# Accumulating DMAs in the FFN of a two-layer hybrid block: y's middle sums and the low part of w_down

## The chip, the cores and the metric

The kernel runs on one core of a Trainium2 chip. The metric is the device time of one execution in microseconds (us). Before the change the median of three runs is 1789.37 us (1785.97 to 1790.05). One core has five engines with queues of their own: TensorE (PE, with its weight loads as PEld), VectorE (DVE), ScalarE (ACT), GpSimd (POOL) and SyncE (SP). DMAs are issued from a queue, in this kernel from SP's and POOL's, and are carried out by 16 DMA engines that all queues share.

## The reference

Two layers work on a main stream x (512 tokens of width 1024) and, in layer 0, on a context stream (256 tokens). Each layer has a mixing part (attention, a Fourier mix and a long convolution) and then the feed-forward part that the change touches:

```python
def conv_ffn(h, w_up, w_c, b_c, w_down):
    u = dwconv3(h @ w_up, w_c, b_c)
    gate, val = jnp.split(u, 2, axis=-1)
    return (jax.nn.silu(gate) * val) @ w_down

fx = rmsnorm(x, g_pre_ffn[i]) * (1.0 + sc2) + sh2
yx = conv_ffn(fx, w_up[i], w_ffn_conv[i], b_ffn_conv[i], w_down[i])
x = x + ga2 * rmsnorm(yx, g_post_ffn[i])
```

`w_up` is 1024 x 5632, `w_down` 2816 x 1024, all in float32. The context stream has the same FFN in layer 0 alone.

## The kernel before

**High and low parts.** A float32 operand of a matmul is split into two tiles of a rounded type (F32R): the high part is the rounded value, the low part the remainder. `split` (lines 179 to 183) does this with a cast on ACT (L181) and a subtraction on DVE or POOL (L182). `mm3` (L196, L197, L198) adds three products into PSUM: high by high, high by low, low by high. `load_w` (L189) loads 512 KB of weights from DRAM to a tile `Wr` on SP's queue and splits it into `Wh` and `Wl`.

**The FFN's loops.** The hidden width is 22 chunks of 128. Per chunk m, the up-projection makes the gate and the value, a convolution over neighbouring tokens follows (`conv3`, L636 to L638), then SiLU on ACT, the product `ft` on POOL (L1229, L1335), and a split into `gc` or `gT`. In the main stream (`ffn_x`) the up-projection is a Strassen-like scheme of seven products. `prep` loads two `w_up` tiles `r` and makes four sums on POOL (`tt`, L1276 to L1279), which are then split into `Wh`, `Wl` and an M tile. In the context stream (`ffn_c`) the `w_up` tiles are split directly (`L`).

**The down-projection.** `ffn_down` takes the chunks in groups of two (the last group of the main stream has four). It loads a group's `w_down` chunks with `load_w`, and for each tile t of 128 tokens it multiplies the group into a PSUM pair `pw` (128 x 1024). The sum over all groups stands in the SBUF tile y[t]: the first group is copied there by ACT (L1200), each middle group is added by DVE (L1202), and the last one is added by halves (L1196), followed by the squares for the norm and the tail (residual, store). A group's down-projection is emitted after the first chunk of the next group. For the context stream the low parts of `w_down` are made on POOL (`CE = True`), for the main stream on DVE: 22 chunks for the context stream and 22 for each layer of the main stream, 66 in all. There are 82 middle sums.

**What sets the order.** In Python, generators yield estimated costs, and a planner (`go`, `pump`, `need`) mixes filler work, such as the modulation matmuls with `w_mod`, into the main work. A scheduler then fixes each engine's own order when the program is built, with a model of time (`schedule_with_timeline_sim=True`, L1698). On the chip each queue runs in that order, and an instruction that waits holds up all behind it on its engine.

**Buffers.** Tiles of one tag share a fixed count of buffers, and a new tile waits until an old one has been read for the last time:

```python
BUFS = {"M": 27, "T": 5, "Q": 3, "L": 3, "Wr": 2, "Wh": 4, "Wl": 4, "Wm": 3}
```

`M` holds y, gT, the Strassen sums and other tiles of 128 x 1024. PSUM has two pairs `pw` and four banks `pn`.

Of the kernel before, what the change touches and what calls it, by code (L numbers as in the profile page):

```python
# [8 lines left out]
F32 = mybir.dt.float32  # L9
F32R = mybir.dt.float32r  # L10
I32 = mybir.dt.int32
AF = mybir.ActivationFunctionType
ALU = mybir.AluOpType
# [4 lines left out]
P = 128  # L18
# [50 lines left out]
class Net:  # L69
# [115 lines left out]
    def load_w(self, src, shape=None, el=None, tag=None, raw=None):  # L185
        shape = shape or [P, 1024]
        r = self.tl(shape, F32, raw or tag or "Wr")
        for i, a in enumerate(src if isinstance(src, list) else [src]):
            self.nc.sync.dma_start(r[:, 2 * i : 2 * i + 2] if isinstance(src, list) else r, a)  # L189
        h, lo = self.tl(shape, F32R, tag or "Wh"), self.tl(shape, F32R, tag or "Wl")  # L190
        self.split(h, lo, r, el)
        return h, lo

    def mm3(self, ps, l, r, first, last, **kw):
# [970 lines left out]
    def ffn_down(self, l, st, g, ms, begin, el=None, early=0, mid=None):  # L1165

        nc = self.nc
        end = ms[-1] == MF - 1
        if begin and st is self.X:
            st.y = [self.M("y", F32) for _ in range(st.NT)]  # L1170
        wd = {k: self.load_w(self.I["w_down"][l, k], el=nc.gpsimd if el else None) for k in ms}
        if end:
            ss = [self.small("ss", 2, 6) for _ in range(st.NT)]
            xr = [self.load_r(self.src[st.name][t]) for t in range(st.NT)]
        acc = {}

        def add(t, h, ks):
            hs, ts = slice(h * 512, (h + 1) * 512), slice(t * P, (t + 1) * P)
            if (t, h) not in acc:
                if h == 0:  # L1180
                    acc[t] = self.pw()
                acc[t, h] = acc[t][:, hs]
            for k in ks:
                self.mm3(acc[t, h], (g[k][:, 0, ts], g[k][:, 1, ts]), (wd[k][0][:, hs], wd[k][1][:, hs]), k == ms[0], k == ms[-1])
            yield 3 * len(ks) * C512, 0.0

        for t in range(early):
            for h in range(2):
                yield from add(t, h, ms[:-1])
        for t in range(st.NT):  # L1190
            y = st.y[t]
            for h in range(2):
                hs = slice(h * 512, (h + 1) * 512)
                yield from add(t, h, ms[-1:] if t < early else ms)
                if end:
                    nc.vector.tensor_tensor(y[:, hs], y[:, hs], acc[t, h], op=ALU.add)  # L1196
                    self.sumsq_half(ss[t], y[:, hs], h)
                    nc.gpsimd.tensor_tensor(y[:, hs], y[:, hs], st.G[1][:, hs], op=ALU.mult)
            if begin:
                nc.scalar.copy(y, acc[t])  # L1200
            elif not end:
                nc.vector.tensor_tensor(y, y, acc[t], op=ALU.add)  # L1202
            else:
                self.tail(st, t, xr[t], ss[t])
                if t == Z["MT"] and mid:
                    yield from mid
# [495 lines left out]
```

## Time and profile before

| | before |
|---|---|
| median of three runs | 1789.37 us |
| profiled execution | 1784.91 us |
| its span (first to last instruction) | 1783.1 us |
| PE busy | 1639.1 us (92%) |
| DVE busy | 1440.1 us (81%) |
| ACT busy | 934.9 us (52%) |
| POOL busy | 692.3 us (39%) |
| DMA queues, share of 16 engines | SP and others 35.6%, POOL 5.5% |

A group row of the profile names the line, engine, operation and tiles (written <- read), the shapes and the count; then busy us and mean ns of one; then the idle time of the engine just before, with what ended it. A wait row names who waited, for whom, total us, times and the longest. A row of a table by stretches has for each engine busy us and count, then TensorE's granted clock, the share of the DMA engines and GB/s. DMA issue rows end with the median us from issue to landing. Rows of the table of DMA queues give packets, MB and the time of the packets as a share of 16 engines' span.

### The profile page before, as it was taken

The page shows a single profiled execution, that of the slowest core. Times are in us where ns is not written, and L with a number is a line of the kernel's source. Part 1 is how long each engine was busy: PE and PEld are TensorE (multiplying, and loading weights), DVE is VectorE, ACT ScalarE, POOL GpSimd, SP SyncE. Part 2 cuts the span into 40 slices and gives each one's busy share as a digit, 9 for nine tenths or more (in the row PEclk, how much of TensorE's full clock was granted, in tenths as well). Part 3 has the DMA queues.
Part 4 walks back from the last instruction along what each step waited for, and adds up shares of the span by engine and source line. Part 5 has one row for each costly group of instructions (what it writes and reads, how often), then busy time and mean ns, then how long its engine had stood idle before and what let it go on. Part 6 is the DMA issues. An engine that isn't in the chain of part 4 may idle for free. (4 is left out here: it accounts for less than half of the span.)

```text
span 1783.1 us, 27842 instructions
## 1 busy us (share of the span) xinstructions
PE 1639.1 (92%) x10502; PEld 1397.4 (78%) x10502; DVE 1440.1 (81%) x2324; ACT 934.9 (52%) x1737; POOL 692.3 (39%) x515
## 2 busy tenths in 40 slices
PE   5799987899999997989999998998898799999997
PEld 2677775687788897878989885787787678889996
DVE  5888777697665688889988987668895878999997
ACT  2642344487565454556554556434773465555454
POOL 3343332000134337665554645212002455655543
PEclk9899999999999998999999999999999899999999
DMA  9214277603477642332342258653012343332323
GB/s 366 101 61 146 86 243 263 232 13 130 162 253 232 228 155 71 96 118 84 101 148 84 89 185 305 213 175 118 1 48 83 130 146 103 95 107 86 127 62 119
DMA packets 70003, 248.01 MB, mean 139 GB/s; under 512 B 8111, under 2 KB 9647, under 8 KB 69868
## 3 DMA queue, kind: packets, MB, share of 16 engines
q1 hardware_dynamic: 60716, 215.54, 35.6%
q0 software_dynamic: 9152, 30.68, 5.5%
q8 instruction: 83, 1.36, 0.3%
q14 instruction: 52, 0.43, 0.1%
HBM read 232.03 MB, written 14.16 MB: 138 GB/s over the span
## 5 line engine op out<-in xcount | busy, mean ns | idle before, releaser
L196 PE MATMUL pn<-h,Wh 128*128 128x256 f32 x1328 | 376.6, 286 | 11.7 <-DVE ft L638 4.3
L198 PE MATMUL pn<-h,Wl 128*128 128x256 f32 x1328 | 372.8, 284 | 10.2 <-DVE Wl L182 10.2
L197 PE MATMUL pn<-h,Wh 128*128 128x256 f32 x1328 | 374.2, 283 | 1.7 <-POOL h L182 1.7
L196 PEld LDWEIGHTS pn<-h,Wh 128*128 128x128 f32 x1328 | 253.2, 191 | 24.5 <-issue 7.8
L198 PEld LDWEIGHTS pn<-h,Wl 128*128 128x128 f32 x1328 | 252.1, 191 | 15.3 <-DVE Wl L182 12.7
L197 PEld LDWEIGHTS pn<-h,Wh 128*128 128x128 f32 x1328 | 253.8, 191 | 6.2 <-POOL h L182 2.4
L181 ACT CAST Wh<-Wr 128x1024 fp32r<-128x1024 f32 x118 | 122.7, 1049 | 138.9 <-PE pw L198 46.4
L182 DVE TENSOR_TENSOR Wl<-Wr,Wh 128x1024 fp32r<-128x1024 f32 x89 | 129.7, 1465 | 53.7 <-ACT Wh L181 53.2
L1276 POOL TENSOR_TENSOR tt<-r,r 128x512 f32<-128x512 f32 x44 | 75.0, 1705 | 233.9 <-DMA r<-w_up 211.0
L196 PE MATMUL pw<-Wh,gT 128*128 128x512 f32 x352 | 137.5, 404 | 9.0 <-ACT gT L181 3.9
L197 PE MATMUL pw<-Wl,gT 128*128 128x512 f32 x352 | 138.5, 396 | 3.1 <-DVE Wl L182 3.1
L198 PE MATMUL pw<-Wh,gT 128*128 128x512 f32 x352 | 137.8, 396 | 1.8 <-DVE gT L182 1.8
L181 ACT CAST Wh<-tt 128x1024 fp32r<-128x1024 f32 x88 | 90.8, 1048 | 84.9 <-PE pn L197 42.4
L182 DVE TENSOR_TENSOR Wl<-tt,Wh 128x1024 fp32r<-128x1024 f32 x88 | 122.5, 1411 | 11.0 <-ACT Wh L181 8.0
L1335 POOL TENSOR_TENSOR ft<-ft,ft 128x512 f32<-128x512 f32 x44 | 70.8, 1609 | 132.4 <-DVE ft L638 94.2
L1202 DVE TENSOR_TENSOR y<-y,pw 128x1024 f32<-128x1024 f32 x82 | 99.2, 1213 | 20.1 <-PE pw L198 20.0
L182 POOL TENSOR_TENSOR h<-tf,h 128x256 fp32r<-128x256 f32 (+1 forms) x40 | 36.0, 921 | 187.8 <-ACT h L181 186.5
L182 POOL TENSOR_TENSOR Wl<-Wr,Wh 128x1024 fp32r<-128x1024 f32 x29 | 74.6, 2578 | 57.7 <-ACT Wh L181 56.5
L1278 POOL TENSOR_TENSOR tt<-r,tt 128x512 f32<-128x512 f32 x44 | 75.8, 1722 | 51.9 <-DVE Wl L182 51.9
L196 PE MATMUL pw<-h,Wh 128*128 128x256 f32 (+1 forms) x224 | 76.9, 343 | 13.9 <-DVE v L638 2.6
L283 PE MATMUL pn<-wm,cpad 128*32 128x256 f32 x768 | 67.6, 411 | 19.7 <-DMA wm<-w_mod 19.3
L636 ACT ACTIVATE ft<-C,vec 128x512 f32<-128x512 f32 x88 | 68.7, 811 | 32.1 <-DVE C L1325 25.7
(361 smaller groups left out, 4706.1 us busy)
## 6 DMA issues: line engine op xcount, KB each, us to landing
wm<-w_mod SPq DMA_DIRECT2D x96, 512.0 KB, 5.4
r<-w_up SPq DMA_DIRECT2D x90, 512.0 KB, 3.6
Wr<-w_down SPq DMA_DIRECT2D x66, 512.0 KB, 3.8
L<-w_up SPq DMA_DIRECT2D x44, 512.0 KB, 4.4
Wr<-w_out SPq DMA_DIRECT2D x24, 512.0 KB, 3.6
Wr<-w_in_t SPq DMA_DIRECT2D x16, 512.0 KB, 3.9
dft<-hdft_x POOLq DMA_DIRECT2D x16, 512.0 KB, 4.1
Wr<-w_in_c SPq DMA_DIRECT2D x12, 512.0 KB, 3.6
```

The costliest lines, as they stand in the source:

```text
L181: r = nc.scalar.copy(hi, src)
L182: (el or nc.vector).tensor_tensor(lo, src, f32(hi), op=ALU.subtract)
L196: nc.tensor.matmul(ps, l[0], r[0], start=first, stop=False, **kw)
L197: nc.tensor.matmul(ps, l[0], r[1], start=False, stop=False, **kw)
L198: nc.tensor.matmul(ps, l[1], r[0], start=False, stop=last, **kw)
L283: nc.tensor.matmul(ps[32 * g : 32 * g + 32, cs], self.cpad[:, q % 2 * 4 + g, :], w[:, g, :], start=q % 2 == 0, stop=q % 2 == 1, skip_group ...
L636: nc.scalar.activation(dst, ps, AF.Identity, scale=w1, bias=b)
L1202: nc.vector.tensor_tensor(y, y, acc[t], op=ALU.add)
L1276: te.tensor_tensor(half(t13, 0), half(r[1], 0), half(r[0], 0), op=ALU.subtract)
L1278: te.tensor_tensor(half(t24, 0), half(r[1], 1), half(t13, 0), op=ALU.subtract)
L1335: nc.gpsimd.tensor_tensor(o[0], o[0], o[1], op=ALU.mult)
```

## The change

Two things are changed in `ffn_down`, for both streams and both layers.

The weights `w_down` are loaded by a new helper, `load_w_acc`. It loads `Wr` as before on SP's queue. ACT then writes the negated, rounded weights to the low tile, and casts the weights to the high tile. A DMA issued on POOL's queue reads the same weights from DRAM a second time and adds them to the low tile, which then holds the weights less the high part. The subtraction on DVE or POOL is gone, so the argument that chose its engine is gone too.

The middle groups' sums are no longer added to y by DVE. ACT copies the PSUM pair to a new M tile `ya`, and a DMA on POOL's queue adds that tile to y, from SBUF to SBUF. The first and last groups stay as they were.

```diff
+    def load_w_acc(self, src):
+
+        nc = self.nc
+        r = self.tl([P, 1024], F32, "Wr")
+        nc.sync.dma_start(r, src)
+        h, lo = self.tl([P, 1024], F32R, "Wh"), self.tl([P, 1024], F32R, "Wl")
+        nc.scalar.activation(lo, r, AF.Copy, scale=-1.0)
+        nc.scalar.copy(h, r)
+        nc.gpsimd.dma_start(lo, src, accum_op=ALU.add)
+        return h, lo
...
-        wd = {k: self.load_w(self.I["w_down"][l, k], el=nc.gpsimd if el else None) for k in ms}
+        wd = {k: self.load_w_acc(self.I["w_down"][l, k]) for k in ms}
...
             if begin:
                 nc.scalar.copy(y, acc[t])
             elif not end:
-                nc.vector.tensor_tensor(y, y, acc[t], op=ALU.add)
+
+                part = self.M("ya", F32)
+                nc.scalar.copy(part, acc[t])
+                nc.gpsimd.dma_start(y, part, accum_op=ALU.add)
             else:
                 self.tail(st, t, xr[t], ss[t])
```

## The prediction

> **What bounds the kernel now.** I began with the stages, because the change touches only the two feed-forward parts. The view of busy time by stretch has, after the stretch and its length, busy us with instruction counts of PE, PEld, DVE, ACT and POOL, then granted clock, DMA share and GB/s. The context stream's FFN lies in 460 to 700 us, the main stream's in 740 to 1090 (layer 0) and 1405 to 1783 (layer 1).
>
> ```profile
> 490.00:624.00 134.00, 134.00 (x970) 116.06 (x969) 85.02 (x127) 73.44 (x113) 52.19 (x35) 1.00 0.71 238
> 740.00:1090.00 350.00, 334.40 (x2214) 298.29 (x2214) 304.92 (x391) 192.15 (x312) 190.12 (x124) 0.99 0.40 133
> 1450.00:1750.00 300.00, 292.38 (x2012) 267.97 (x2012) 270.68 (x297) 160.74 (x250) 155.02 (x93) 0.99 0.33 106
> ```
>
> PE is busy 100%, 96% and 97% of these stretches at a granted clock of 0.99 or 1.00. The timeline says that this is real issue and not only modelled ends: consecutive 256-column matmuls start every 0.12 us.
>
> ```profile
> 1519.74 0.28 PE L197 MATMUL pn<-h,Wh 128*128 128x256 f32 x1
> 1519.86 0.28 PE L198 MATMUL pn<-h,Wl 128*128 128x256 f32 x1
> 1519.98 0.28 PE L196 MATMUL pn<-h,Wh 128*128 128x256 f32 x1
> ```
>
> DVE is the second load (85 of 134, 305 of 350, 271 of 300), ACT and POOL are near half. So relief of DVE is worth only what PE waits for DVE. The waits of PE in the three stages (total us, times, longest), one block of rows a stage in the order 460 to 700, 740 to 1090, 1405 to 1783:
>
> ```profile
> PE pn L196 <- DVE ft L638: 4.3, 1, 4.3
> PE pn L198 <- DVE Wl L182: 2.9, 2, 1.6
> ...
> PE pw L196 <- ACT gT L181: 3.1, 3, 2.0
> PE pw L197 <- DVE Wl L182: 3.1, 2, 2.0
> PE pn L198 <- DVE Wl L182: 2.4, 4, 1.0
> PE pw L198 <- DVE gT L182: 0.9, 1, 0.9
> ...
> PE pn L198 <- DVE Wl L182: 4.1, 3, 2.5
> PE pw L196 <- DVE y L1196: 1.7, 2, 1.2
> PE pn L196 <- DVE C L1323: 1.1, 3, 0.7
> ```
>
> Waits of PE that end with DVE in these rows sum to 4.3 + 2.9 + 3.1 + 2.4 + 0.9 + 4.1 + 1.7 + 1.1 = 20.5 us. That is the largest direct gain that I can point to.
>
> **The change, part by part.** What it takes away and what it adds is priced from these groups (busy us, mean ns of one; two windows for the subtraction of the main stream, one for the context stream):
>
> ```profile
> L182 DVE TENSOR_TENSOR Wl<-Wr,Wh 128x1024 fp32r<-128x1024 f32 x22 | 36.7, 1677 | 2.9 <-ACT Wh L181 2.9
> L182 DVE TENSOR_TENSOR Wl<-Wr,Wh 128x1024 fp32r<-128x1024 f32 x22 | 36.9, 1697 | 0.5 <-ACT Wh L181 0.4
> L182 POOL TENSOR_TENSOR Wl<-Wr,Wh 128x1024 fp32r<-128x1024 f32 x20 | 51.3, 2573 | 46.7 <-ACT Wh L181 46.5
> L1202 DVE TENSOR_TENSOR y<-y,pw 128x1024 f32<-128x1024 f32 x82 | 99.2, 1213 | 20.1 <-PE pw L198 20.0
> L181 ACT CAST Wh<-Wr 128x1024 fp32r<-128x1024 f32 x118 | 122.7, 1049 | 138.9 <-PE pw L198 46.4
> L1200 ACT COPY y<-pw x10: 1002/1008/1017, 508.7 to 1470.7; 128x1024 f32<-128x1024 f32 x10
> L716 POOL DMA_DIRECT2D dft<-hdft_x x16 | 9.5, 597 | 50.1 <-PE pn L198 43.6 <-DVE dec L750 3.6 <-PE pn L791 0.8
> Wr<-w_down SPq DMA_DIRECT2D x66, 512.0 KB, 3.8
> dft<-hdft_x POOLq DMA_DIRECT2D x16, 512.0 KB, 4.1
> ```
>
> - DVE loses 44 subtractions and 82 additions, 73.6 + 99.2 = 173 us of its 1440. POOL loses 22 subtractions of 2.57 us (57 us) and gains 66 + 82 = 148 DMA issues of 0.60 us (88 us). ACT gains 66 negated copies of 1.05 us and 82 copies out of PSUM of 1.01 us, 152 us, which puts it near 70% in the FFN.
> - **DVE's relief.** At most the 20.5 us above; those waits also have other causes in the same chains (the cast ahead of Wl, the POOL product ahead of gT), so I take half: −10 us (bounds −21 and 0).
> - **y's middle sums.** The PSUM pair was freed after an addition of 1.21 us and is now freed after a copy of 1.01 us: nothing lost there. The DMA behind it has a whole group (some 30 us) until y is touched again, so its landing costs 0. It waits on POOL for ACT's copy. Queued behind it are the four `tt` operations of the next weights and the product `ft`, for which ACT's cast of gT waits and then PE. POOL has idle time there before the first of these, so I take 0; without that cover it is at most 82 waits of one copy, 82 x 1.01 = 83 us:
>
> ```profile
> L1276 POOL TENSOR_TENSOR tt<-r,r 128x512 f32<-128x512 f32 x44 | 75.0, 1705 | 233.9 <-DMA r<-w_up 211.0
> L1335 POOL TENSOR_TENSOR ft<-ft,ft 128x512 f32<-128x512 f32 x44 | 70.8, 1609 | 132.4 <-DVE ft L638 94.2
> ```
>
> (`part` holds one of the 27 M buffers for a copy and a landing, some 5 us; whether one is free is not shown, I take 0 inside the same bound.)
>
> - **w_down's low part** is the term that decides. Before it was made by a subtraction behind the cast; now it is a negated copy, an issue in POOL's queue, and a landing. One group in layer 1, main stream:
>
> ```profile
> 1547.62 1.06 ACT L181 CAST Wh<-Wr 128x1024 fp32r<-128x1024 f32 x1
> ...
> 1548.36 2.24 POOL L1276 TENSOR_TENSOR tt<-r,r 128x512 f32<-128x512 f32 x1 [3.72 <-DVE Wl L182]
> ...
> 1550.04 1.65 DVE L182 TENSOR_TENSOR Wl<-Wr,Wh 128x1024 fp32r<-128x1024 f32 x1
> ...
> 1552.89 0.40 PE L197 MATMUL pw<-Wl,gT 128*128 128x512 f32 x1
> ```
>
> Before, Wl is ready at 1551.69 and PE reads it at 1552.89, 1.2 us later. After, the negated copy ends at 1548.68, POOL is in a `tt` until 1550.60, and a plain 512 KB load issued by POOL lands 4.1 us after its issue starts: 1554.7, or 1.8 us after PE used it. An accumulating DMA has to read the destination too. No row shows one. Its lower bound is the plain load; its upper bound is two plain passes. The size of a pass follows from the DMA table:
>
> ```profile
> q1 hardware_dynamic: 60716, 215.54, 35.6%
> q0 software_dynamic: 9152, 30.68, 5.5%
> ```
>
> POOL's queue took 5.5% of 1783 us, 98 us of all 16 engines, for 30.68 MB, so 0.524 MB take 1.7 us. With a second pass Wl is late by 1.8 + 1.7 = 3.5 us. I take the middle, 2.65 us. PE does other matmuls meanwhile: in the group shown it ran products of the next weights between its first matmul on the new Wh and that on Wl. But those products need buffers too: Wh and Wl have four each, a down group keeps two of them some 20 us, and ACT already waits for them (138.9 us before the casts in the group above). So a longer stay is partly paid later, by casts that start late. I take half of 2.65 us for each of 20 down groups of the main stream (ten a layer): +27 us (bounds 0 and 20 x 3.5 = 70). In the context stream PE never idled between 490 and 624 us, and the subtraction that falls away there cost 2.57 us itself; I take 0 for its latency, and the same 11 x 3.5 = 39 us as upper bound.
>
> - **DMA load in the context stream.** 20 chunks of w_down and 16 middle sums fall into 460 to 700 us:
>
> ```profile
> L181 ACT CAST Wh<-Wr x20: 1046/1048/1057, 494.1 to 672.1; 128x1024 fp32r<-128x1024 f32 x20
> L1202 DVE TENSOR_TENSOR y<-y,pw 128x1024 f32<-128x1024 f32 x16 | 19.5, 1219 | 6.9 <-PE pw L198 6.8
> ```
>
> That is 36 DMAs more, 60 us of all engines by one pass, spread over 240 us: +0.25 of the share, +0.50 by two passes. In 490 to 624 us the share is 0.71 already, so it becomes 0.96 to 1.21, 1.085 in the middle. What is over 1.00 lengthens the 134 us: 0.085 x 134 = +11 us (bounds 0 and 28). What is late next there is `L`, the w_up loads. In the main stream 0.40 and 0.33 leave room: 0.
>
> By the Trainium skill, "Collectives: The Full Stack", section "The bandwidth ceiling: the fold count and why AG ≠ RS ≠ AR", an adding transfer runs at half the rate of a copy, since each chunk needs two reads on one ring and the addition itself is free. By that rule the delay would be 3.5 us and the terms +35 and +28 in place of +27 and +11, an estimate 25 us higher; no trace here shows it.
>
> **The sum.** −10 + 27 + 11 = +28 us. The profiled execution took 1784.9 us (its span is 1783.1, 1.8 us lie around it), so 1813 us. The median of the runs shown is 4.5 us above that execution; the sum put on the median would be 1817, and I name 1815.
>
> **The rivals.**
>
> *Faster: the latency is covered and DVE's relief is left.* The scheduler that writes the order knows a DMA takes time and can put the loads ahead. Place: the pair Wl of w_down. It decides if PE has at least 3 us of `pn` products at hand for each group, which the timeline of the group above supports; the buffers' waits speak against. Price: all of DVE's 20.5 us with nothing paid, and 5 to 10 us more from DVE operations that no longer run beside each other: 1789 − 21 = 1768 to 1789 − 10 = 1779; I name 1774.
>
> *No difference: PE bound.* PE issues at its rate in 96% and more of these stretches. Then neither the 173 us that DVE loses nor a delay of 2 to 3 us reaches the end. 1789 us.
>
> *Much slower: an accumulating DMA lands as late as the slow loads in POOL's queue.* The four reloads of `h` landed after 8.3 to 14.1 us:
>
> ```profile
> h<-spill_h POOLq DMA_DIRECT2D x4, 512.0 KB, 11.1
> ```
>
> With 11.1 in place of 4.1 us, Wl is late by 8.8 us in each group. Half of it over 20 groups is 88 us, half over the 11 groups of the context stream 48 us, and the DMA load adds its upper 28 us: 1789 + 164 − 10 = 1943 at worst, and 1789 + 88 + 11 − 10 = 1878 if PE, always at work in the context stream, hides that stream's part. Those four loads came in one burst, which speaks against it.
>
> *The change does not do what it says*, if the addition were carried out by several small transfers or on POOL itself. Then POOL's issue would be longer than 0.6 us; at 1.7 us (a `tt`) 148 issues are 163 us more on an engine that is idle nearly half of the FFN: it ends within the much slower case.
>
> **How the numbers follow.** A measurement of this kernel tells apart about 0.2%, 3.6 us. Chances: forecast 0.45 (own range 1797 to 1843: between a third of the delay paid with no DMA overload, 1789 − 10 + 18, and all of it, 1789 − 10 + 53 + 11), much slower with its variants 0.18, faster 0.26, no difference 0.11. Slower by over 0.2% is 0.45 + 0.18 = 0.63, same 0.11, faster 0.26. Against the sum speaks that only PE decides, for it that every added step stands in a chain whose slack is 1.2 us. The range takes in the faster case's 1768 and the milder half of the much slower one, 1880: about 0.1 is left out on either side.
>
> **What would show it.** In the changed profile: waits of PE on a DMA into Wl (right if 10 us or more in all, wrong if none); the landing of the accumulating DMA from DRAM between 4.1 and 5.8 us, and POOL's issue near 0.6 us; the DMA share of the context stream at 0.95 or more, and waits for `L` there; DVE's busy time near 1440 − 173 = 1267 us or somewhat lower, ACT's near 1087; the stretch of the main stream's FFN longer in both layers. The forecast is wrong if PE's busy share in those stretches stays at 96% or more and their length does not grow, or if most of a loss sits in POOL's `ft`, behind y's DMAs, which I priced at 0.

## The result and the profile after

| | before | after |
|---|---|---|
| median | 1788.56 us | 1938.85 us (1931.65 to 1943.01) |
| ratio to before, 95% interval | | 1.0838 [1.0801, 1.0875] |
| span of the profiled execution | 1783.1 us | 1929.9 us |

The kernel is 8.4% slower. Forecast were 1815 us in a range of 1768 to 1880: the direction came out, the size did not. In the changed kernel the lines stand some ten further down: the matmuls L196, L197, L198 are now L207, L208, L209, the negated copy is L200, the cast of `w_down` L201, its accumulating DMA L202, y's copy L1215 and y's DMA L1216. The split stays at L181 and L182.

The page of after, its engines and its DMA queues:

```profile
PE 1685.2 (87%) x10502; PEld 1429.8 (74%) x10502; DVE 1302.5 (67%) x2198; ACT 1069.5 (55%) x1885; POOL 715.7 (37%) x641
...
q1 hardware_dynamic: 60716, 215.54, 31.6%
q0 software_dynamic: 30464, 108.29, 27.0%
```

PE was busy 92% of the span and is now busy 87%. DVE lost 138 us (1440 to 1302), less than the 173 forecast, and POOL's queue moves 108 MB in place of 31.

Where the time went is seen from marks that both kernels have (the first store of x, the last `w_up` split of the context stream, the stores of layer 0, the last store). The context stream's FFN grew from 223.0 to 255.1 us, the main stream's from 392.7 to 458.1 (layer 0) and 411.9 to 462.2 (layer 1). The mixing part between the two stayed (285.2 and 283.9). So the three FFN stages hold the whole difference: 32 + 65 + 50 = 147 us. The waits of PE in after (us in total, times, longest):

```profile
PE pw L208 <- DMA Wl<-w_down: 101.7, 34, 7.0
PE pn L294 <- DMA wm<-w_mod: 22.1, 16, 5.4
PE pn L207 <- ACT Wh L181: 10.6, 10, 2.1
...
PE pn L209 <- DVE Wl L182: 7.7, 8, 4.2
```

The first row answers the row `PE pw L197 <- DVE Wl L182` of before, 3.1 us in the three stages. 34 times PE stood for 3 us on average before the low part of `w_down`. The stretches (after the length: busy us of PE, PEld, DVE, ACT, POOL, then granted clock, DMA share, GB/s), which answer the three at the head of the prediction:

```profile
490.00:635.00 145.00, 129.27 (x896) 110.04 (x895) 65.55 (x107) 84.45 (x124) 33.93 (x40) 0.95 0.93 275
740.00:1180.00 440.00, 375.94 (x2433) 335.47 (x2432) 268.51 (x349) 256.09 (x381) 227.53 (x187) 0.93 0.69 177
1500.00:1900.00 400.00, 348.45 (x2286) 312.46 (x2286) 261.60 (x296) 234.43 (x341) 209.97 (x166) 0.94 0.67 168
```

PE's share is 89%, 85% and 87% where it was 100%, 96% and 97%; the granted clock went from 0.99 or 1.00 to 0.93 to 0.95; and the DMA share of the main stream rose from 0.40 and 0.33 to 0.69 and 0.67. The landings in after, median us in the last column:

```profile
r<-w_up SPq DMA_DIRECT2D x90, 512.0 KB, 5.9
y<-ya POOLq DMA_DIRECT2D x82, 512.0 KB, 6.0
Wr<-w_down SPq DMA_DIRECT2D x66, 512.0 KB, 6.6
Wl<-w_down POOLq DMA_DIRECT2D x66, 512.0 KB, 7.9
L<-w_up SPq DMA_DIRECT2D x44, 512.0 KB, 7.4
```

### The profile page after: what moved, and what is told of

It reads as the page before. It is cut to its first block, busy times and chain, and to the rows that moved or that the text cites. A ratio compares the mean times of both kernels' runs of the same rounds, so it can differ in the third digit from the quotient of the medians.

```text
span 1929.9 us, 28251 instructions
## 1 busy us (share of the span) xinstructions
PE 1685.2 (87%) x10502; PEld 1429.8 (74%) x10502; DVE 1302.5 (67%) x2198; ACT 1069.5 (55%) x1885; POOL 715.7 (37%) x641
## 5 line engine op out<-in xcount | busy, mean ns | idle before, releaser
L207 PE MATMUL pn<-h,Wh 128*128 128x256 f32 x1328 | 382.9, 290 | 17.4 <-ACT Wh L181 10.6
L209 PE MATMUL pn<-h,Wl 128*128 128x256 f32 x1328 | 376.0, 289 | 7.8 <-DVE Wl L182 7.7
L208 PE MATMUL pn<-h,Wh 128*128 128x256 f32 x1328 | 378.7, 287 | 1.7 <-POOL h L182 1.7
L207 PEld LDWEIGHTS pn<-h,Wh 128*128 128x128 f32 x1328 | 260.0, 196 | 29.7 <-ACT Wh L181 13.8
L209 PEld LDWEIGHTS pn<-h,Wl 128*128 128x128 f32 x1328 | 257.7, 197 | 15.0 <-DVE Wl L182 10.0
L208 PEld LDWEIGHTS pn<-h,Wh 128*128 128x128 f32 x1328 | 259.4, 195 | 6.4 <-POOL h L182 2.0
L208 PE MATMUL pw<-Wl,gT 128*128 128x512 f32 x352 | 150.0, 426 | 78.7 <-DMA Wl<-w_down 78.7
L182 DVE TENSOR_TENSOR Wl<-tt,Wh 128x1024 fp32r<-128x1024 f32 x88 | 126.2, 1440 | 41.1 <-ACT Wh L181 41.1
L207 PE MATMUL pw<-Wh,gT 128*128 128x512 f32 x352 | 144.4, 419 | 3.9 <-DVE y L1207 1.9
L209 PE MATMUL pw<-Wh,gT 128*128 128x512 f32 x352 | 146.3, 417 | 0.0
L208 PEld LDWEIGHTS pw<-Wl,gT 128*128 128x128 f32 x352 | 69.8, 198 | 98.6 <-DMA Wl<-w_down 84.1
L1215 ACT COPY ya<-pw 128x1024 f32<-128x1024 f32 x82 | 82.7, 1012 | 81.2 <-PE pw L209 81.0
L181 ACT CAST Wh<-tt 128x1024 fp32r<-128x1024 f32 x88 | 91.8, 1050 | 54.3 <-POOL tt L1293 37.7
L182 DVE TENSOR_TENSOR Wl<-r,Wh 128x1024 fp32r<-128x1024 f32 x40 | 70.2, 1754 | 68.6 <-ACT Wh L181 68.5
L648 DVE SCALAR_TENSOR_TENSOR ft<-C,vec,ft 128x511 f32<-128x511 f32 x88 | 84.8, 992 | 37.7 <-ACT ft L647 37.7
L649 DVE SCALAR_TENSOR_TENSOR ft<-C,vec,ft 128x511 f32<-128x511 f32 x88 | 107.0, 1251 | 0.2
L182 POOL TENSOR_TENSOR h<-tf,h 128x256 fp32r<-128x256 f32 (+1 forms) x40 | 37.5, 958 | 187.0 <-ACT h L181 183.1
L1216 POOL DMA_DIRECT2D y<-ya x82 | 74.3, 933 | 84.9 <-ACT ya L1215 71.5
L182 DVE TENSOR_TENSOR Wl<-L,Wh 128x1024 fp32r<-128x1024 f32 x44 | 58.3, 1326 | 68.3 <-ACT Wh L181 68.2
L181 ACT CAST Wh<-Wr 128x1024 fp32r<-128x1024 f32 x52 | 54.3, 1050 | 85.8 <-PE pw L209 45.6
L182 DVE TENSOR_TENSOR Wl<-Wr,Wh 128x1024 fp32r<-128x1024 f32 x45 | 56.1, 1249 | 50.4 <-ACT Wh L181 50.1
```

The costliest lines, as they stand in the source:

```text
L181: r = nc.scalar.copy(hi, src)
L182: (el or nc.vector).tensor_tensor(lo, src, f32(hi), op=ALU.subtract)
L207: nc.tensor.matmul(ps, l[0], r[0], start=first, stop=False, **kw)
L208: nc.tensor.matmul(ps, l[0], r[1], start=False, stop=False, **kw)
L209: nc.tensor.matmul(ps, l[1], r[0], start=False, stop=last, **kw)
L648: nc.vector.scalar_tensor_tensor(dst[:, 1:T], ps[:, 0 : T - 1], w0, dst[:, 1:T], op0=ALU.mult, op1=ALU.add)
```

## Experiments

Four explanations were set against each other: the low part lands late and nothing covers it; the added transfers and issues load the DMA engines and POOL; ACT's added copies cost; the four `Wh` and four `Wl` buffers turn round more slowly.

### Which part of the change

y's sums alone (`w_down` as before):

```diff
-        wd = {k: self.load_w_acc(...) for k in ms}
+        wd = {k: self.load_w(..., el=nc.gpsimd if el else None) for k in ms}
```

> Only y's middle sums go through ACT's copy and the accumulating DMA; w_down's low part is made by the subtraction as before. Theory A (PE waits for w_down's late low part, and little else costs): between -10 and +20 us against the kernel before, no wait of PE on a DMA into Wl. Theory B (the load of the 148 accumulating DMAs and of the copies on DMA engines, ACT and POOL): 82 of 148 DMAs, so some +80 us of the +146.

Measured 1813.58 us, 1.0128 [1.0098, 1.0157]. And `w_down`'s low part alone (y's sums by DVE as before):

```diff
-                part = self.M("ya", F32)
-                nc.scalar.copy(part, acc[t])
-                nc.gpsimd.dma_start(y, part, accum_op=ALU.add)
+                nc.vector.tensor_tensor(y, y, acc[t], op=ALU.add)
```

> Only w_down's low part is made by the negated copy and the accumulating DMA; y is summed by DVE as before. Theory A: +120 to +150 us, with PE's waits on the DMA into Wl near the 102 us of the changed kernel. Theory B: 66 of 148 DMAs, some +65 us.

Measured 1940.15 us, 1.0839 [1.0795, 1.0884]: as much as the whole change. So `w_down`'s part alone is enough for a loss of this size, and y's part, which costs 25 us alone, adds nothing to the total. By the marks the two runs are not the same, though: `w_down` alone has 237.4 us in the context stage and 464.8 and 475.6 in the main ones, where the whole change has 255.1, 458.1 and 462.2. y's sums on top cost 18 us in the context stage and give 20 back in the main ones; that these cancel is luck. Waits of PE in the run with y's sums alone:

```profile
PE pn L209 <- DVE Wl L182: 19.8, 18, 5.7
...
PE pw L207 <- ACT ya L1215: 9.7, 13, 2.0
```

No wait of PE on y's DMA is among them. The PSUM pair is now freed by ACT's copy, and PE waits for that 13 times; the waits of this kind for DVE's `Wl` have doubled (10.2 us, 10 times, in the whole run of before). y's copy without its DMA (the middle sums are then missing in y):

```diff
                 nc.scalar.copy(part, acc[t])
-                nc.gpsimd.dma_start(y, part, accum_op=ALU.add)
```

> The kernel with y's sums alone changed, without the accumulating DMA: ACT copies the middle groups' sums to the M tile and they are dropped (the middle sums are left out of y). If the +25 us of y's change come from the DMAs (issue, waits in POOL's queue, DMA engines): 0 to -15 us against the kernel before, since DVE's 99 us are gone. If they come from ACT's copy in the path that frees the PSUM pair: +15 to +30 us.

Measured 1803.65 us, 1.0076 [1.0053, 1.0098]. About 13 us of the 25 are there with the copy alone, although DVE has lost its 82 additions and has nothing in their place.

### Accumulating or plain

The same kernel with a plain DMA into the low tile, so that the high part is not subtracted:

```diff
-        nc.gpsimd.dma_start(lo, src, accum_op=ALU.add)
+        nc.gpsimd.dma_start(lo, src)
```

> As the kernel with w_down's low part alone changed, but the DMA of POOL's queue writes the weights over the low tile in place of adding them (the low tile then holds the whole weights, so the subtraction of the high part is left out). Same places in every queue, no second read. Theory A: the landing falls from 5.3 us at best to about 4 us, PE's waits on Wl fall by that much in each of some 34 waits, so 40 to 60 us less than with the addition, but still slower than before. Theory B: the share of the DMA engines falls by 66 x 1.2 us, so at most 10 us less.

Measured 1841.94 us, 1.0286 [1.025, 1.0321]. The built order of every engine is the same in this run and in that of `w_down` alone, instruction by instruction, so the 98 us between them are what adding costs over copying, and nothing else. That is more than either expectation gave. POOL's issue (ns min/median/max), first in the accumulating kernel:

```profile
L202 POOL DMA_DIRECT2D Wl<-w_down x66: 850/874/1609, 501.4 to 1898.8; - x66
```

and in the plain one:

```profile
L202 POOL DMA_DIRECT2D Wl<-w_down x66: 527/584/599, 498.2 to 1801.7; - x66
...
Wl<-w_down POOLq DMA_DIRECT2D x66, 512.0 KB, 6.0
...
PE pw L208 <- DMA Wl<-w_down: 43.5, 20, 6.0
```

The accumulating kernel has the medians 0.87 us and 8.6 us and the following waits of PE:

```profile
PE pw L208 <- DMA Wl<-w_down: 104.7, 32, 7.1
```

So 61 of the 98 us are PE's direct waits. One group of the accumulating kernel shows the rest. ACT first:

```profile
1733.97 0.37 ACT L1309 COPY C<-pn 128x256 f32<-128x256 f32 x1 [1.88 <-PE pn L209]
1735.97 1.05 ACT L201 CAST Wh<-Wr 128x1024 fp32r<-128x1024 f32 x1 [1.62 <-PE pn L208]
1736.92 1.05 ACT L200 ACTIVATE Wl<-Wr 128x1024 fp32r<-128x1024 f32 x1
1737.88 1.03 ACT L201 CAST Wh<-Wr 128x1024 fp32r<-128x1024 f32 x1
1738.82 1.05 ACT L200 ACTIVATE Wl<-Wr 128x1024 fp32r<-128x1024 f32 x1
```

Then POOL's issues and SP's in the same time:

```profile
1738.28 0.88 POOL L202 DMA_DIRECT2D Wl<-w_down  x1 [0.79 <-ACT Wl L200]
1740.17 0.86 POOL L202 DMA_DIRECT2D Wl<-w_down  x1 [1.01 <-ACT Wl L200]
...
1738.00 2.22 SPq L198 DMA_DIRECT2D Wr<-w_down  x2
```

And PE:

```profile
1740.94 0.28 PE L209 MATMUL pn<-h,Wl 128*128 128x256 f32 x1
1744.73 0.80 PE L208 MATMUL pw<-Wl,gT 128*128 128x512 f32 x1 [3.51 <-DMA Wl<-w_down]
1745.32 0.63 PE L209 MATMUL pw<-Wh,gT 128*128 128x512 f32 x1
...
1747.46 0.41 PE L207 MATMUL pn<-h,Wh 128*128 128x256 f32 x1
1747.67 0.42 PE L208 MATMUL pn<-h,Wh 128*128 128x256 f32 x1
```

The chain of the group starts when PE releases a `Wh` buffer (L208 ahead of the cast; the weights themselves had landed some 30 us earlier). Four operations of ACT follow in a row. POOL issues the first DMA at 1738.28; PE is at the first product on `Wl` at 1741.06 (0.12 us after its last start), 2.8 us later; the DMA lands at 1744.69. In the plain kernel PE comes as early (2.7 us after the issue) and the DMA lands 4.6 us after its issue. The negated copy also frees `Wr`, and SP's next two loads go out at that moment, beside the DMAs on which PE waits. The stretches of this group in the accumulating kernel, before the stall, the stall, and the time behind it:

```profile
1725.00:1741.00 16.00, 16.00 (x124) 15.36 (x122) 9.45 (x11) 9.46 (x13) 8.70 (x6) 1.00 0.33 98
1741.00:1744.70 3.70, 0.22 (x2) 0.02 (x1) 3.52 (x5) 2.55 (x6) 1.09 (x2) 0.89 1.01 223
1744.70:1750.70 6.00, 5.97 (x22) 5.40 (x23) 0.00 (x0) 1.14 (x2) 1.25 (x2) 0.50 0.80 216
1750.70:1755.00 4.30, 4.30 (x28) 3.88 (x28) 3.99 (x6) 2.24 (x3) 2.25 (x2) 1.00 0.02 6
```

Two things are to be seen. The DMA engines are full during the stall (1.01); their share was 0.33 before it, is 0.80 in the 6 us behind it, and falls to 0.02 only then. And PE comes back at a granted clock of 0.50 for 6 us: 256-column matmuls start every 0.21 us in place of 0.12. A stall of 3.7 us so costs about 3 us more behind it. The same stretches in the plain kernel:

```profile
1624.50:1627.20 2.70, 2.70 (x23) 2.60 (x21) 0.41 (x1) 2.70 (x4) 1.11 (x3) 1.00 0.77 223
1627.20:1629.10 1.90, 0.20 (x2) 0.00 (x0) 1.90 (x4) 1.90 (x6) 0.00 (x0) 1.00 1.01 326
1629.10:1635.00 5.90, 5.86 (x30) 5.53 (x31) 2.34 (x5) 2.62 (x5) 2.02 (x1) 0.71 0.69 242
```

Here the stall is 1.9 us, and the clock afterwards 0.71 on average (1.00 at first, then 0.50 from 1630.5 to 1633.9). I added up, over each trace from 460 us on, the excess of those matmuls that start 1.5 to 2.2 times the undisturbed distance (0.117 us for 256 columns, 0.234 for 512) after their predecessor. It is 39.4 us before, 67.0 after, 72.3 for `w_down` alone, and 47.6 with the plain DMA. Between the accumulating and the plain kernel that is 25 us, which with the 61 makes 86 of the 98. The granted clock of the same traces gives somewhat more: half of PE's busy time at 0.50 is 26 us before, 69 after, 76 for `w_down` alone and 42 with the plain DMA, so 34 us between the last two, and with the 61 it makes 95 of the 98. Of 21 stalls of 3.5 us or more in the accumulating kernel, 16 were followed by more than 1 us at the half rate, from the second matmul on at the latest; of 63 stalls of 0.5 to 3.5 us, 8 were.

This group is of the kernel with `w_down`'s part alone. In the changed kernel the low part is late by another link in most of the main stream. One of its groups, ACT, POOL and PE:

```profile
1692.83 1.07 ACT L200 ACTIVATE Wl<-Wr 128x1024 fp32r<-128x1024 f32 x1
...
1698.08 1.72 POOL L1290 TENSOR_TENSOR tt<-r,r 128x512 f32<-128x512 f32 x1 [11.17 <-DVE ft L648]
1699.77 1.74 POOL L1291 TENSOR_TENSOR tt<-r 128x512 f32<-128x512 f32 x1
1701.45 0.88 POOL L202 DMA_DIRECT2D Wl<-w_down  x1
...
1706.87 0.59 PE L208 MATMUL pw<-Wl,gT 128*128 128x512 f32 x1 [4.93 <-DMA Wl<-w_down]
```

The first negated copy ended at 1693.90, and POOL was idle. But its queue held two `tt` operations ahead of the DMA, and the first of them waited until 1698.08 for a product of DVE, so the DMA was issued 7.6 us after the copy. PE was at its product 0.3 us later, and the DMA took 5.4 us. In 14 of the 20 main-stream groups the issue came 3.8 to 9.0 us after the copy in this way, behind `tt` operations that in most cases waited for the `w_up` loads; 59 of PE's 101.7 us fall into these groups. With `w_down` alone the issue followed the copy by 0.3 us in the median, and the landing was longer (8.6 us in the median, 7.9 in the changed kernel). No run moves the DMA ahead of the `tt` in the changed kernel, so what this place in the queue costs there is not shown.

### Load, and ACT's copy

The kernel before, with the negated copy and the accumulating DMA made beside it into an M tile that nobody reads:

```diff
+        x = self.M("wx")
+        nc.scalar.activation(x, r, AF.Copy, scale=-1.0)
         self.split(h, lo, r, el)
+        nc.gpsimd.dma_start(x, src, accum_op=ALU.add)
```

> The kernel before, and beside its subtractions a negated copy of each w_down chunk into an M tile and an accumulating DMA onto it, which nobody reads (this work is added, no result of it is used). Theory A: the load alone costs little, 0 to +30 us, and PE has no wait on such a DMA. Theory B: at least the cost of the w_down part, +65 us or more.

Measured 1893.16 us, 1.0579 [1.0553, 1.0606]. Even unread they cost 105 us, though PE cannot wait for that DMA; it waits for ACT's casts instead (28.2 + 19.8 us). That is the second expectation's price; the next runs take it apart. The same without the DMA:

```diff
-        nc.gpsimd.dma_start(x, src, accum_op=ALU.add)
```

> The kernel with the unread accumulating DMAs, without these DMAs: what is left beside the kernel before is a negated copy of each w_down chunk by ACT into an M tile that nobody reads (work added, not used). If the copy, its M tile and the longer hold of Wr made the +105 us: +50 to +100 us. If the DMAs made it: 0 to +20 us.

Measured 1853.13 us, 1.0345 [1.0318, 1.0373]. Two of its waits of PE:

```profile
PE pw L205 <- ACT Wh L181: 29.1, 8, 11.8
...
PE pn L205 <- ACT Wh L181: 8.0, 7, 3.4
```

66 copies of 1.05 us (69 us of an engine that is busy 54%) cost 62 us or so. Some of this is the M tile: the kernel before with only its low tile moved to M, a control for a later run, measured 1815.57 us, 1.0148 [1.0107, 1.0189].

The transfers alone: the kernel before, with 66 accumulating DMAs from `w_down` to a scratch tensor in DRAM.

```diff
+        nc.gpsimd.dma_start(dst, src, accum_op=ALU.add)
```

> The kernel before, and for each of the 66 w_down chunks an accumulating DMA on POOL's queue from the weights in DRAM onto a scratch tensor in DRAM (work added, its result is not used). No ACT copy, no tile, no wait before it. It shows the load of the DMA engines and of POOL's issue alone. If that load made the +105 us of the unread DMAs: +60 us or more. If it was the negated copy and the tiles it holds: 0 to +25 us.

Measured 1930.22 us, 1.0787 [1.0767, 1.0807], but this run missed its purpose: nothing tied the DMAs to their place, and the scheduler put all of them at the start of the kernel. The first mark moved from 466.6 to 614.5 us, and the FFN stages stayed (221.2, 394.0 and 413.1 us). The same with each DMA tied behind a product `ft` on POOL:

```diff
+        with self.tc.issue_after(self.fp):
+            self.nc.gpsimd.dma_start(dst, src, accum_op=ALU.add)
```

> The 66 accumulating DMAs from w_down onto a scratch tensor in DRAM once more (added work, result not used), but each held on POOL's queue behind a product ft of the FFN, so that they run in the FFN and not at the start. Theory C (the FFN's rate is set by how long a weight tile takes from the release of its Wh or Wl buffer to its use, and work beside that chain is free): 0 to +20 us. Theory D (load of the DMA engines and of POOL's queue): +60 us or more, with DMA-late weights.

Measured 1807.77 us, 1.0102 [1.0061, 1.0143]; context stage 221.2, main stages 403.3 and 414.7. 66 such transfers in the FFN cost 18 us when nobody waits for them and they hold no tile. Between the two runs with the unread copy the DMA cost 42 us (1.0579 less 1.0345); there it also holds an M tile until it lands. So load that nobody waits for is a small part of the 150 us. What the same load adds to a landing on which PE does wait is not in these runs, and their target is DRAM in place of SBUF.

`w_down` alone with the negated copy on DVE:

```diff
-        nc.scalar.activation(lo, r, AF.Copy, scale=-1.0)
+        nc.vector.tensor_scalar(lo, r, -1.0, None, op0=ALU.mult)
```

> The kernel with w_down's low part alone changed, with the negated copy made by DVE in place of ACT; the cast stays on ACT. Theory C: ACT no longer delays the cast and the next weights by 1.05 us a chunk, which cost up to the 62 us of the negated copies alone: 30 to 60 us less than that kernel's +152, waits of PE on the DMA remain. Theory D: no change, within 15 us.

Measured 1884.37 us, 1.0526 [1.0473, 1.058]: 56 us less than with the copy on ACT. PE's waits fall from 104.7 to 69.1 us, and the excess at half rate from 72.3 to 54.5.

```profile
PE pw L208 <- DMA Wl<-w_down: 69.1, 45, 5.6
```

The copy on ACT, but written behind the cast in place of ahead of it:

```diff
-        nc.scalar.activation(lo, r, AF.Copy, scale=-1.0)
         nc.scalar.copy(h, r)
+        nc.scalar.activation(lo, r, AF.Copy, scale=-1.0)
```

> w_down's low part by the accumulating DMA alone (y's sums as before), with ACT's two operations swapped: the cast to Wh first, the negated copy second. All other engines keep their order. If the negated copy costs because it holds up the cast (Wh and what follows it on ACT), the waits behind ACT's cast fall and the time falls by up to the 56 us that its move to DVE saved: about 1885 to 1900. If the landing of Wl is the last to come in each group, the DMA now starts one copy (1.05 us) later and the time rises by about 32 to 45 times 1.05, 35 to 45 us: about 1975 to 1985.

Measured 1937.48 us, 1.0835 [1.0795, 1.0875], as with `w_down` alone. The edit changed next to nothing in the program: the scheduler had already put the cast first for nearly all chunks (as in the group above), whatever the text said, and with the swapped text it built the same order on every engine but for three pairs on ACT. So this run shows nothing of which of the two should go first, and neither expectation was tested.

The copy on DVE and the plain DMA together:

> The negated copy on DVE, and a plain DMA in place of the accumulating one (so the high part is not subtracted in Wl; the products are otherwise the same). With the copy on ACT the plain DMA saved 98 us. If ACT's copy and the accumulating DMA's longer way are two prices that add up, this run is near 1884 - 98 = 1786, as before. If they are one price (the later of two links in the same chain decides), the plain DMA saves less than half of that here and the run is at 1840 or more.

Measured 1802.07 us, 1.0075 [1.0054, 1.0097]. Its order is again that of the accumulating kernel with the copy on DVE, instruction by instruction. PE's waits on the low part are nearly gone:

```profile
PE pw L208 <- DMA Wl<-w_down: 12.4, 11, 2.5
```

So the loss of `w_down`'s part comes apart, from ratios times 1789: 13 us remain with both replaced, ACT's copy adds 38 by a plain DMA (56 by an accumulating one), and adding in place of copying adds 98 with the copy on ACT (81 with it on DVE). Along one way through these runs the steps make up the whole loss by construction (13 + 38 + 98 = 149 of 150). What the four runs show beyond that is that the two prices overlap: each is some 17 us larger beside the other. The 1802 us lie nearer to the first expectation, two prices that add up. The copy's move to DVE also changes the built order, so its price is that of the reordered program.

### Cover, buffers, lead

More work ahead of the low part: the whole change, with the high-part products of two token tiles first and those with `Wl` last (some 3.7 us of cover).

```diff
+            if not end and t % 2 == 0:
+                for a in (t, t + 1):
+                    for h in range(2):
+                        yield from wh(a, h)
...
+                yield from (add(...) if end else wl(t, h))
```

> The changed kernel, with the order of the products in the first and the middle down groups changed: for two token tiles first all products with the high part of w_down (16 matmuls of 0.23 us, 3.7 us), then those with the low part. Nothing else is changed. Theory A (PE reaches a product with the low part before it has landed and has no other work): PE's waits on the DMA into Wl fall from 102 us to under 40, and the time by 50 to 90 us. Theory B (load on the engines and DMA): within 15 us of the changed kernel.

Measured 1938.4 us, 1.0816 [1.0782, 1.0851]: no gain. PE still waits 81.6 + 12.2 us for the DMA into `Wl`. The built order explains part of it:

```profile
1847.81 2.00 ACT L200 ACTIVATE Wl<-Wr 128x1024 fp32r<-128x1024 f32 x2
...
1855.78 0.87 POOL L202 DMA_DIRECT2D Wl<-w_down  x1
...
1861.20 1.22 PE L1214 MATMUL pw<-Wl,gT 128*128 128x512 f32 x2 [6.18 <-DMA Wl<-w_down]
```

The copies had ended at 1849.81, but in POOL's queue the DMA again stood behind `tt` operations, and PE was at its product 0.9 us before the issue. In such a group the added products stand ahead of the issue and cover nothing. So this run does not show what 3.7 us between issue and use are worth.

The low tile in M, to free `Wl` buffers (in all groups but the last):

```diff
-        h, lo = self.tl([P, 1024], F32R, "Wh"), self.tl([P, 1024], F32R, "Wl")
+        h, lo = self.tl([P, 1024], F32R, "Wh"), self.M("wl")
```

> The kernel with w_down's low part alone changed, with that low part in a buffer of the M tiles in place of Wl, for all groups but the last (whose four do not fit). The same copies and DMAs, but they need not wait for a Wl buffer and do not keep one from w_up. Theory C: PE's waits on the DMA fall from 105 us to under 50, and the time by 50 to 110 us. Theory D: no change, within 15 us.

Measured 1956.6 us, 1.0953 [1.0898, 1.1007]. Its control, the kernel before with the same edit:

> Control: the kernel before with w_down's low part in an M buffer in place of Wl, for all groups but the last; the subtraction stays. Theory C: 0 to -15 us, since its chain is short already. If M buffers are scarce in the FFN: slower by 10 us or more, and the same cost is in the run with the DMA.

Measured 1815.57 us, as said. Net of the control `w_down`'s part costs 144 us there (1.0953 less 1.0148) in place of 150, so freeing `Wl` is worth little. This does not clear the buffers altogether: what the casts in the group above waited for was `Wh`, which this edit does not free.

Lead: `w_down` alone, with the loads, copies and DMAs of the main stream written one chunk ahead.

```diff
+                wd = {k: self.load_w_acc(...) for k in groups[i - 1]} if i and j == 0 else None
                 yield from rest(m)
```

> w_down's low part by the accumulating DMA alone, in the main stream with the group's two w_down loads written ahead of the seven products of the chunk before (a lead of some 10 us of PE's work). If the loss is lead time that the order did not give (PE comes 2.7 us after the issue), PE's waits for the DMA into Wl go from 105 us to under 30 in the main stream and the time to 1850 to 1880. If the four Wh and four Wl buffers set the pace, the waits move to ACT's casts of the w_up weights (ACT Wh) and the time stays at 1920 or rises.

Measured 1903.22 us, 1.0639 [1.0611, 1.0666]. And with a smaller lead, inside the chunk, ahead of the next chunk's weights:

> As the run before with a smaller lead: the two loads are written inside the chunk's products, just ahead of the next chunk's w_up weights, so that they take their buffers before those do. Lead time: waits for the DMA into Wl under 30 us in the main stream, 1850 to 1880. Buffers: the w_up weights come later by as much, 1920 or more.

Measured 1902.36 us, 1.0628 [1.0577, 1.0679]. Both gain some 37 us and no more; PE's waits are still 85.3 and 81.8 us. They lie between the two expectations. Here too the weights of `w_down` had landed some 30 us before the copy, which still stood behind casts to `Wh` in ACT's order. The last pair takes the low part out from behind that release: load, negated copy and DMA one chunk ahead into an M tile, the cast to `Wh` where it was.

```diff
+    def cast_w(self, r, lo):
+        h = self.tl([P, 1024], F32R, "Wh")
+        self.nc.scalar.copy(h, r)
+        return h, lo
```

> w_down's low part by the accumulating DMA alone; in the main stream (all groups but the last) the load, the negated copy and the accumulating DMA are written one chunk ahead, into an M tile, and only the cast to Wh stays where it was. So the low part no longer waits for the release of a Wh buffer. If the loss is that the landing stands in the loop from PE's release of a Wh buffer over ACT's cast, the copy and the DMA back to PE, then PE's waits for the DMA in the main stream fall from some 80 us to under 20, and the time to about 1830 to 1865 (what is left: the context stream's 14, the M tile's 20 to 25, ACT's copies). If instead there is no ready work for PE anyway (the four buffers set the pace, and the waits only change their name), the time stays at 1900 or above, with waits behind ACT's casts (ACT Wh) in their place.

Measured 1915.05 us, 1.0712 [1.0675, 1.0748]; with the copy on DVE:

> As the run before with the negated copy on DVE. If ACT's copy is a price of its own, this takes another 40 to 56 us: 1785 to 1820, near the 1815 of the kernel before with its low tile in M. If ACT's copy cost only because it stood in the loop ahead of the DMA, the two runs agree within 10 us.

Measured 1898.67 us, 1.0625 [1.0589, 1.0661]. Waits of PE in the first:

```profile
PE pw L212 <- DMA wl<-w_down: 43.8, 17, 7.5
...
PE pw L212 <- DMA Wl<-w_down: 28.3, 17, 5.2
```

In four of these 18 groups the first low part was now really early (one was issued at 1636.92, landed at 1642.54 and was used at 1651.49). In most others it was not (issued at 1682.61, landed at 1688.39, used at 1688.43). Rather more than half of the main stream's waits are left (43.8 of some 80 us). The time lies where the second expectation had it, at 1900 or above, but without its sign: PE's waits behind ACT's casts to `Wh` are 12.4 us. With the copy on DVE the run is 16 us faster, between its two expectations. Why the order keeps most of the copies late, and why a run with 72 us of waits is still 100 us above its control of 1815, stays open. None of the versions beats the kernel before.

## Why the prediction failed

**The step that failed is the term of `w_down`'s low part (+27 us).** It measured about 150 us. Five pieces of its working were off; the prices of the copies and of the adding DMA come from the kernel with `w_down`'s part alone.

- *The queue.* The working had one `tt` in POOL's queue ahead of the issue, 1.9 us after the copy ("POOL is in a `tt` until 1550.60"). In 14 of 20 main-stream groups of the changed kernel it was 3.8 to 9.0 us. The DMA stood behind `tt` operations that were themselves waiting, in order.
- *The cover.* "PE does other matmuls meanwhile ... I take half of 2.65 us." The order of the engines is fixed when the program is built. In the changed kernel it brought PE to the low part 0.3 to 3.4 us after POOL's issue in most groups of layer 1, and in the kernel with `w_down` alone 2.7 to 2.8 us, whether the DMA then needed 4.6 us or 6.4. What the landing took beyond that was waited for in full: 34 waits of 3.0 us.
- *The landing.* Forecast were 4.1 to 5.8 us; it was 5.3 at best and 7.9 in the median. In the 14 groups with the late issue the first DMA mostly took 5.3 to 5.8, within the forecast; in the context stream the median was 10.2. The plain DMA in the same place took 3.9 and 6.0 beside 5.3 and 8.6. The issue took 0.88 us in place of 0.60. The term took a landing in a quiet stretch. With `w_down` alone the copy frees `Wr`, and the next loads collide with the DMA: "In the main stream 0.40 and 0.33 leave room: 0" was read from an average; in the stall shown the share was 1.01.
- *ACT's copies.* "ACT gains 66 negated copies of 1.05 us" was given no price. ACT is near half busy, but its casts start at PE's release of a buffer, and the copies stand in that chain. Their move to DVE was worth 56 us with the accumulating DMA and 38 with the plain one, in the kernel with `w_down`'s part alone. The working also let the copy start in the cast's place; the built order put the cast first.
- *The clock.* The prediction counted a stall as lost time and no more. After a stall of some 3.5 us PE came back at half rate, 27.6 us in all over before (67.0 less 39.4). With the direct waits of 101.7, in place of 3.1, that is 126 of the 147 us; by the granted clock it is 43 us, and 142 of the 147. The Trainium skill, "TensorE: Matmul & The Clock Gate", section "HAM oscillation — how this bites in real kernels", says that idle gaps over about 3.4 us bring the clock to half. The trace agrees (a stall of 3.7 us, then 0.50 for 6 us), and the plain kernel's 1.9 us, with 0.71 behind it, shows that a shorter stall can be followed by it too. The forecast's delay of 2.65 us lay below that limit and its upper bound of 3.5 us at it; the waits came out longer.

**The context stream's latency**, "I take 0", was wrong as well: PE stood 20.4 us there for `Wl`, nine times, and the stage grew by 32 us.

**The DMA load of the context stream (+11).** The share came to 0.93 between 490 and 635 us, not over 1, with `L` landing in 7.4 us in place of 4.4. ACT's waits for `L` in this stage rose from 1.5 to 10.6 us. But the tied transfers left that stage at 221 us with a share of 0.81 over the whole stage (0.85 after), so load alone is not shown to lengthen it. With `w_down` alone the stage grew by 14 us of the 32; what the other 18 are, which came with y's sums, stays open.

**The DVE's relief (−10).** No run shows it. y's additions taken from DVE without a DMA in their place made the kernel slower by 13 us, and giving DVE the 66 copies made it faster by 56.

**y's sums at 0.** Right in the total beside `w_down`'s part (1938.85 against 1940.15 us), by luck: +18 us in the context stage and −20 in the main ones. Alone they cost 25 us. Its DMA was no direct wait of PE, as forecast. The cost fell elsewhere than feared: not on POOL's `ft`, but on the PSUM pair ("nothing lost there" cost 9.7 us of waits on ACT's copy); 13 of the 25 us came with the copy alone.

**The two-pass rule.** By the Trainium skill, "Collectives: The Full Stack", section "The bandwidth ceiling: the fold count and why AG ≠ RS ≠ AR", the adding transfer runs at half rate. POOL's queue took 27.0% of 1929.9 us less the 98 us of before, 423 us for 148 DMAs: 2.86 us of all engines each, 1.7 times a plain one. In the two kernels with the same order the queue took 14.5% of 1937.0 us and 10.8% of 1837.6; less the same 98 us, that is 2.77 us for each of the 66 DMAs when adding and 1.52 when copying, 1.8 times. The rule is close, but it added 25 us to a forecast that was short by 124.

**The rivals.** The result lies inside the "much slower" case (1878 to 1943), to which 0.18 was given. Its place was right and its price was not: the landing was 7.9 us rather than 11.1, and the late issue, the missing cover, ACT and the clock made up for it. "Faster" and "no difference" both rested on PE having other products at hand or setting the pace alone; the busy shares of 85 to 89% exclude that. The variant in which the addition is carried out on POOL falls with the issue of 0.88 us (1.7 was its price).

**What would show it.** Waits of PE on a DMA into `Wl` over 10 us, longer main stages in both layers, waits for `L` in the context stream and ACT near 1087 us (1069.5) came as said. The landing, the share of 0.95, the issue near 0.6 and DVE at 1267 or lower (1302.5) did not.

## What to carry to other kernels

Before an operation is replaced by a DMA, read from the timeline what stands ahead of it in the issuing queue and how long after its issue the bound engine comes to the result, and compare that with a landing beside the transfers that start at the same moment; in these runs, with their fixed order, the difference was waited for in nearly every round. Price an added operation by the chain in which it stands, not by its engine's busy share: on ACT, busy about half the time, the copies still cost 56 us. And look at the granted clock behind each stall of PE, because long stalls are paid there a second time.

## What the runs showed of the hardware

An accumulating DMA of 512 KB from DRAM to SBUF took 2.77 us of all 16 engines against 1.52 for a plain one, 0.87 us of POOL's issue against 0.58, and landed after 5.3 us at best against 3.9 in the same places. In the traces here PE's granted clock is 0.50 for some 6 us after a stall of 3.7 us, and 16 of 21 stalls of 3.5 us or more were followed by more than 1 us of it. Two programs with the same order on every engine differed by 98 us through the kind of 66 DMAs alone.
